# Routed experts of a mixture-of-experts layer: two output sums instead of one, and what is moved with them

## The chip, the cores and the metric

The kernel runs on one core of a Trainium2 chip. The metric is device time in microseconds (us) of one launch; the median of three runs of the kernel before is 2050.76 us (2043.1 to 2051.07). The kernel is written in an explicit form: each engine (TensorE for matmuls, VectorE, ScalarE and GpSimd for element work, SyncE for issuing DMAs) carries out its own list of instructions in order, and engines wait for each other and for DMAs on semaphores, which a tile layer derives from the reads and writes of each tile or DRAM tensor.

## The reference

One decoder layer on 1024 tokens of width 1024, all in float32: a mixing part (a state-space branch and a sparse-attention branch), and then a mixture of experts whose end is what the change touches:

```
scores = sigmoid(h @ w_router)               # 64 experts, top 8 of them per token, group-limited
w      = chosen scores / their sum * 2.5
for each expert e, for its tokens t:
    hid      = silu(h[t] @ w_gate[e]) * (h[t] @ w_up[e])      # 1024 -> 256
    routed[t] += (hid @ w_down[e]) * w[t, e]                   # 256 -> 1024
shared = (silu(h @ ws_gate) * (h @ ws_up)) @ ws_down
out    = x + gate_f * (routed + shared)
```

So every row of the output is a sum of ten terms: the residual x, the shared expert's row, and eight experts' rows.

## The kernel before

The sum is kept in the output tensor in DRAM itself. The mixing part writes x there. The shared expert's down projection (`job_down`, line 1735) works in eight groups of 128 rows and adds each group with a DMA that accumulates (line 1759). The routed experts (`moe`, line 2099) then add their rows one block at a time.

A block is up to 128 tokens of one expert. Experts are ranked by their number of tokens; a table (`SLOTS`, line 27) gives each rank one, two or three blocks of fixed sizes, 98 blocks in all: 38 of 128 rows, 12 of 64, 4 of 48, 26 of 88 to 120, and 18 of 32 rows or fewer (5 of 8, 5 of 16, 4 of 24, 4 of 32). `moe_order` (line 2026) puts seven experts with one block first, then mixes experts with one and with more blocks, and ends on the largest experts and three small ones. [...] The order within the loop is written out by hand (lines 2234 to 2273); for block b it is, on all engines together:

- `gu(b)`: gate and up projection on TensorE. Blocks over 64 rows use weights and tokens split in a high and a low part (three matmuls each, lines 253 to 255); smaller ones use plain float32 with the array cut into two or four column groups, so that two or four matmuls run beside each other (line 2169).
- `gather(b + 3)` (line 1858): an indirect DMA, issued by GpSimd, that brings the tokens of a later block into one of three buffers.
- `put(b - 2)`: VectorE multiplies the down projection's result with the token weights and the gate into one of two output buffers (line 2222; for up to 64 rows ScalarE first copies one half, line 2221), and GpSimd issues an indirect DMA that adds the rows to the output (line 2223, the scatter). Indices are distinct within one block but not between blocks, so each scatter waits until the one before has landed.
- `ht(b - 1)`: transposes of the hidden values (lines 2188 and 2191); `act(b)`: the SwiGLU (lines 2177 and 2178); `xpose(b + 2)`: transposes of the gathered tokens (lines 2141 and 2150); `dn(b - 1)`: the down projection (line 2210), four matmuls of 512 columns, for up to 64 rows in two column groups of the array.
- in between, the high and low parts of the next expert's weights (lines 2090 and 2091, on ScalarE and VectorE), and at the end of an expert the weight loads for three experts ahead (3 MB, lines 2068 and 2078, issued by SyncE).

GpSimd's list in this phase is therefore gather, scatter, gather, scatter, and it holds in order: a gather behind a scatter that waits is not issued either. Lists of each expert's tokens are still being made in the first blocks (`take` and `merge`), as much as the gathers of larger experts require.

Of the kernel before, what the change touches and what calls it, by code (L numbers as in the profile page):

```python
# [10 lines left out]
F32 = mybir.dt.float32  # L11
F32R = mybir.dt.float32r
BF = mybir.dt.bfloat16
I32 = mybir.dt.int32
AF = mybir.ActivationFunctionType
OP = mybir.AluOpType
# [4 lines left out]
P = 128  # L21
T = 1024
D = 1024
# [98 lines left out]
class Kernel:  # L122
# [1612 lines left out]
    def job_down(self):  # L1735

        nc, S = self.nc, self.sh
        ys = {}

        def grp(i, h):  # L1740
            def f(ws):
                ps = self.ps("mm", "mm")
                t = slice(i * P, (i + 1) * P)
                for j in range(2):
                    for k in range(2):
                        self.mm3(ps[:, 256 * j:256 * j + 256], S["hh"][:, k, t], S["hl"][:, k, t], *ws[4 * h + 2 * j + k],
                                 k == 0, k == 1)

                def after():
                    if h == 0:  # L1750
                        ys[i] = self.e1.tile([P, D], F32, name="y", **(dict(tag="mwT") if i % 3 == 2 else dict(tag="y", bufs=2)))
                    c = slice(512 * h, 512 * h + 512)
                    if h == 0:
                        nc.vector.tensor_tensor(ys[i][:, c], ps, self.r_gf[:, c], op=OP.mult)
                    else:
                        nc.scalar.copy(ys[i][:, c], ps)
                        nc.gpsimd.tensor_tensor(ys[i][:, c], ys[i][:, c], self.r_gf[:, c], op=OP.mult)
                    if h == 1:
                        nc.gpsimd.dma_start(self.out[i * P:(i + 1) * P], ys[i], accum_op=OP.add)
                return after  # L1760
            return f
        return (self.I["ws_down"], KT, 256, [grp(i + x, h) for i in range(0, KT, 2) for h in range(2) for x in range(2)])
# [336 lines left out]
    def moe(self):  # L2099
        nc, I, fp, rp = self.nc, self.I, self.fp, self.rp  # L2100
        v = nc.vector
        mm = nc.tensor.matmul
        W, order = self.W, self.order
        r4 = self.r4
        r3, gates = self.r3, self.gt

        c = 3 * (D + 64)
        self.spare, self.nov = r3[:64, c:c + 640], r3[:1, c + 640:c + 641].bitcast(I32)
        hT = self.qp.tile([P, 2, 2, P], F32, name="hT", tag="qb")
        xhs = [self.qp.tile([P, 4, 280], F32R, name="xh", tag="wraw", bufs=2) for _ in range(2)]  # L2110
        xhs = [x.rearrange("p k n -> p (k n)")[:, :D].rearrange("p (k n) -> p k n", k=KT) for x in xhs]
        ots = [r4[:, i * D:(i + 1) * D] for i in range(2)]
        self.keysF = r4[:64, 2 * D:3 * D]

        xss = [r4[:, 2 * D + 512 * i:2 * D + 512 * i + 512] for i in range(2)]
        nc.gpsimd.memset(r4[:, 2 * D:3 * D], 0.0)
        hids = self.hids = [r4[:, 3 * D + 256 * i:3 * D + 256 * i + 256] for i in range(2)]
        self.ov = r4[:1, 3 * D + 512:4 * D].bitcast(I32)
        wts, self.cols = [gates[:, i:i + 1] for i in range(6)], gates[:64, 8:24]
        gf = self.gf = self.r_gf  # L2120
        depth, nr = sum(QUOTA[0]), [sum(len(x) > q for x in QUOTA) for q in range(3)]
        r0, _ = self.first_ranks()
        bg = self.take(self.taken, depth) + [lambda: self.merge(depth, [(0, 0, r0), (1, 0, nr[1]), (2, 0, nr[2])])]
        tables = self.overflow_tables()
        bg, left = bg + tables, len(tables)
        blocks, B = self.blocks, self.B
        nb = len(blocks)
        def units(e):
            return [lambda k=k: self.gu_part(e, k, v) for k in range(len(W[e]["gu"]), KT)]

        def xpose(b):
            s = B[b]
            n, x = s["n"], s["x"]
            s["w"] = wts[b % 6][:n]
            v.tensor_copy(s["w"], x[:, D + s["r"]:D + s["r"] + 1])
            if n <= 64:
                m = s["m"] = 32 if n <= 32 else 64
                xs = xss[b % 2].rearrange("p (k n) -> p k n", k=KT)
                ps = self.ps("xt", "tp", [P, KT, 64])[:, :, :n]
                for k in range(KT):  # L2140
                    nc.tensor.transpose(ps[:, k], x[:, k:D:KT], self.ident[:n, :n])
                nc.scalar.copy(xs[:, :, :n], ps)
                s["st"] = [xs[:, k, :m] for k in range(KT)]
                return
            hi, lo = xhs[b % 2][:, :, :n], fp.tile([P, KT, P], F32R, name="xl", tag="xl", bufs=2)[:, :, :n]
            s["st"] = [(hi[:, k], lo[:, k]) for k in range(KT)]
            for q in range(2):
                ps = self.ps("xt", "tp", [P, 4, P])[:, :, :n]
                for k in range(4):
                    nc.tensor.transpose(ps[:, k], x[:, 4 * q + k:D:KT], self.ident[:n, :n])  # L2150
                ks = slice(4 * q, 4 * q + 4)
                nc.scalar.copy(hi[:, ks], ps)
                v.tensor_tensor(lo[:, ks], ps, hi[:, ks].bitcast(F32), op=OP.subtract)
# [46 lines left out]
        def dn(b):  # L2200

            s = B[b]
            n, w, st = s["n"], W[s["e"]]["dn"], s["hst"]
            if n > 64:
                s["o"] = [self.ps("o", "mm")[:n] for _ in range(2)]
            else:
                ps = self.ps("o", "mm")
                s["o"] = [ps[:n], ps[64:64 + n]]
            for k, h in [(k, h) for h in range(2) for k in range(2)] if n > 64 else [(k, h) for k in range(2) for h in range(2)]:
                mm(s["o"][h], st[:, k], w[:, k, 512 * h:512 * h + 512], start=k == 0, stop=k == 1)  # L2210

        def put(b):
            s = B.pop(b)
            n = s["n"]
            ot = ots[b % 2][:n]
            for h in (1, 0):
                c = slice(512 * h, 512 * h + 512)
                o = s["o"][h]
                if n <= 64 and h == 1:
                    o = ot[:, c]  # L2220
                    nc.scalar.copy(o, s["o"][1])
                v.scalar_tensor_tensor(ot[:, c], o, s["w"], gf[:n, c], op0=OP.mult, op1=OP.mult)  # L2222
            nc.gpsimd.indirect_dma_start(out=self.out, out_offset=bass.IndirectOffsetOnAxis(ap=s["ix"], axis=0),  # L2223
                                         in_=ot, in_offset=None, compute_op=OP.add)

        ne = len(order)
        xpose(0)
        for f in units(0):
            f()
        xpose(1)  # L2230
        for f in self.w_load(2, nc.sync):
            f()
        queue = []
        for b in range(nb + 2):
            if b < nb:
                e, r, q, n, first, last = blocks[b]
                if first:
                    assert not queue
                    if e + 1 < ne:
                        queue = units(e + 1)  # L2240
                    turns = len(QUOTA[r]) if e + 1 < ne else 1
                gu(b)
            if b + 3 < nb:
                while blocks[b + 3][1] < r0 and len(bg) > left:
                    bg.pop(0)()
                self.gather(b + 3)
            if 0 <= b - 2:
                put(b - 2)
            if b < nb:
                take = -(-len(queue) // max(turns, 1))  # L2250
                na = (take * 2 + 2) // 3
                for _ in range(na):
                    queue.pop(0)()
                if b > 0:
                    ht(b - 1)
                act(b)
                if b + 2 < nb:
                    xpose(b + 2)
                if b > 0:
                    dn(b - 1)  # L2260
                for _ in range(take - na):
                    queue.pop(0)()
                turns -= 1
                if last:
                    if e + 3 < ne:
                        for f in self.w_load(e + 3, nc.sync):
                            f()
                for _ in range(2 if 0 < b < self.rate[0] else b < self.rate[1] or b % 2):
                    if bg:
                        bg.pop(0)()  # L2270
            elif b == nb:
                ht(b - 1)
                dn(b - 1)
# [4 lines left out]
    def run(self):  # L2278
        nc, tc = self.nc, self.tc
        with ExitStack() as top:  # L2280
# [4 lines left out]
            self.d_u = self.dp.tile([512, T], F32, name="d_u")  # L2285
            self.d_ma = self.dp.tile([1024, T], F32, name="d_ma")
            self.d_h2 = self.dp.tile([T, D + 64], F32, name="d_h2")
            self.d_mask = self.dp.tile([64, T], F32, name="d_mask")
            self.fp = None
            self.idx0 = cp.tile([P, 64], I32, name="idx0")  # L2290
# [148 lines left out]
```

## Time and profile before

| what | value |
|---|---|
| median of three runs | 2050.76 us (2043.1 to 2051.07) |
| the profiled execution | 2056.37 us |
| its span, first to last instruction | 2054.6 us |
| mean granted TensorE clock | 0.963 |
| TensorE busy | 1910.8 us, 93% of the span |
| VectorE, ScalarE, GpSimd busy | 62%, 43%, 33% |
| bytes moved by DMA | 396 MB, mean 193 GB/s |

Busy TensorE is counted from the first to the modelled end of each matmul, and matmuls overlap, so "busy" says that it had work, not that it ran at its peak. The granted clock is a share of 2.4 GHz; a stretch between 0.5 and 1.0 has a part at 1.2 GHz. "Landing" of a DMA is the time from its issue until its semaphore says that all data are there. In the views, POOL is GpSimd, PE TensorE, DVE VectorE, ACT ScalarE, and a name such as `out<-ot,idx` gives the tensor written and those read (`idx` and `back` are two tables of token indices: those of an expert's first block, and of its later ones). A bracket `[9.46 <-DMA out<-ot,idx]` gives the idle time before an instruction and what ended it.

### The profile page before, as it was taken

The numbers are of one execution on the slowest core, as the hardware profiler recorded it, in microseconds if no ns is written. First come the engines' busy times: TensorE is split into PE (matmuls) and PEld (weight loads), VectorE is DVE, ScalarE is ACT, GpSimd is POOL, SyncE is SP. The second block draws the span as 40 slices with busy tenths as digits, with TensorE's granted clock in tenths as the row PEclk, the third lists the DMA queues.
The fourth block names the chain that finished last, engine by engine and source line by source line (L and its number), as shares of the span: only waits on it lengthen the run. The fifth ranks groups of instructions, "written<-read, shape, count | busy, mean of one in ns | idle before, by whom it ended". The sixth has DMA issues, their size and how long they took to land. (4 is left out here: it accounts for less than half of the span.)

```text
span 2054.6 us, 31808 instructions
## 1 busy us (share of the span) xinstructions
PE 1910.8 (93%) x11227; PEld 1381.7 (67%) x11227; DVE 1278.2 (62%) x2875; ACT 874.7 (43%) x2113; POOL 677.2 (33%) x706
## 2 busy tenths in 40 slices
PE   5997999999899999999898999999999999999897
PEld 4785887889866655688776565666666666666563
DVE  5740694256778886557778765656665655656454
ACT  5221224125667666333334444444444444444332
POOL 7524231222032111234436334433332323323231
PEclk9998999999979999999999999999999999999998
DMA  8327430731023210464349998898989989989984
GB/s 289 92 83 89 106 101 26 239 96 42 22 83 104 71 53 21 151 214 154 134 144 250 367 294 303 270 300 304 299 288 313 300 290 294 308 291 311 278 233 110
DMA packets 150420, 396.31 MB, mean 193 GB/s; under 512 B 22049, under 2 KB 89298, under 8 KB 125666
## 3 DMA queue, kind: packets, MB, share of 16 engines
q1 hardware_dynamic: 117330, 288.28, 40.1%
q0 software_dynamic: 25152, 87.10, 18.8%
q10 hardware_dynamic: 7776, 18.88, 2.5%
q8 instruction: 89, 1.46, 0.3%
q14 instruction: 73, 0.60, 0.1%
HBM read 328.27 MB, written 64.23 MB: 191 GB/s over the span
## 5 line engine op out<-in xcount | busy, mean ns | idle before, releaser
L289 POOL TENSOR_TENSOR wlo<-wraw,whi 128x256 fp32r<-128x256 f32 (+1 forms) x238 | 198.2, 854 | 435.8 <-ACT whi L288 428.1
L2091 DVE TENSOR_TENSOR gl<-raw,gh 128x512 fp32r<-128x512 f32 x508 | 325.4, 688 | 22.5 <-ACT gh L2090 22.2
L2210 PE MATMUL o<-rawdn,hT 128*128 128x512 f32 (+10 forms) x784 | 312.2, 628 | 4.6 <-ACT hT L2189 4.5
L2090 ACT CAST gh<-raw 128x512 fp32r<-128x512 f32 x512 | 280.8, 628 | 13.2 <-DMA raw<-in_w_gu 13.2
L2223 POOL DMA_INDIRECT out<-ot,idx x64 | 115.6, 1806 | 368.1 <-DMA out<-ot,idx 122.0
L253 PE MATMUL gu<-gh,xh 128*128 128x512 f32 (+5 forms) x512 | 220.1, 430 | 0.0
L2222 DVE SCALAR_TENSOR_TENSOR ot<-o,wts,r_gf 128x512 f32<-128x512 f32 (+11 forms) x162 | 115.0, 742 | 152.8 <-DMA out<-ot,idx 66.2
L254 PE MATMUL gu<-gl,xh 128*128 128x512 f32 (+5 forms) x512 | 202.5, 395 | 0.0
L255 PE MATMUL gu<-gh,xl 128*128 128x512 f32 (+5 forms) x512 | 202.3, 395 | 0.0
L2210 PEld LDWEIGHTS o<-rawdn,hT 128*128 128x128 f32 (+10 forms) x784 | 105.5, 164 | 132.5 <-issue 118.8
L255 PE MATMUL mm<-hT_hi,wlo 128*128 128x512 f32 x352 | 141.0, 401 | 18.1 <-POOL wlo L289 18.1
L288 ACT CAST whi<-wraw 128x256 fp32r<-128x256 f32 (+1 forms) x264 | 95.8, 405 | 138.4 <-DMA wraw<-in_w_in 44.4
L253 PE MATMUL mm<-hT_hi,whi 128*128 128x512 f32 x352 | 142.1, 404 | 0.3 <-ACT hT_hi L467 0.3
L254 PE MATMUL mm<-hT_lo,whi 128*128 128x512 f32 x352 | 140.1, 398 | 0.2 <-DVE hT_lo L474 0.2
L253 PEld LDWEIGHTS gu<-gh,xh 128*128 128x128 f32 (+5 forms) x512 | 93.0, 182 | 56.5 <-issue 33.1
L2223 POOL DMA_INDIRECT out<-ot,back x34 | 57.9, 1704 | 215.7 <-DMA out<-ot,idx 160.7
L254 PEld LDWEIGHTS gu<-gl,xh 128*128 128x128 f32 (+5 forms) x512 | 93.0, 182 | 31.9 <-issue 7.9
L255 PEld LDWEIGHTS gu<-gh,xl 128*128 128x128 f32 (+5 forms) x512 | 92.6, 181 | 27.0
L2169 PE MATMUL gu<-raw,ot 128*32 128x128 f32 (+1 forms) x1664 | 100.2, 312 | 0.0
L1332 POOL TENSOR_TENSOR p<-p,ms 128x384 f32<-128x384 f32 (+7 forms) x52 | 45.7, 895 | 165.2 <-DVE ms L1325 86.7
L1318 ACT ACTIVATE p<-p,ms 128x384 f32<-128x384 f32 (+7 forms) x128 | 85.9, 673 | 32.6 <-DVE ms L1312 32.2
L2189 ACT COPY hT<-ht 128x256 f32<-128x256 f32 (+5 forms) x64 | 22.8, 356 | 180.5 <-PE ht L2188 180.0
(580 smaller groups left out, 4166.4 us busy)
## 6 DMA issues: line engine op xcount, KB each, us to landing
raw<-in_w_gu SPq DMA_DIRECT2D x124, 1024.0 KB, 10.1
rawdn<-in_w_down SPq DMA_DIRECT2D x62, 1024.0 KB, 11.2
wraw<-in_w_ada SPq DMA_DIRECT2D x32, 512.0 KB, 3.7
wraw<-in_w_in SPq DMA_DIRECT2D x28, 512.0 KB, 4.3
ada<-in_w_ada SPq DMA_DIRECT2D x16, 512.0 KB, 8.5
d_th<-th ACTq DMA_DIRECT2D x32, 256.0 KB, 2.0
wraw<-in_w_out SPq DMA_DIRECT2D x16, 512.0 KB, 4.6
x<-in_x SPq DMA_DIRECT2D x8, 512.0 KB, 6.4
```

The costliest lines, as they stand in the source:

```text
L253: mm(ps, lh, rh, start=start, stop=False)
L254: mm(ps, lh, rl, start=False, stop=False)
L255: mm(ps, ll, rh, start=False, stop=stop)
L288: self.nc.scalar.copy(hi, raw)
L289: (eng or self.nc.gpsimd).tensor_tensor(lo, raw, hi.bitcast(F32), op=OP.subtract)
L1318: nc.scalar.activation(p, p, AF.Exp, scale=-1.0, bias=m[:, nch - 1, h:h + 1], accum_out=m[:, 3, h:h + 1])
L2090: self.nc.scalar.copy(hi, src)
L2091: eng.tensor_tensor(lo, src, hi.bitcast(F32), op=OP.subtract)
L2169: mm(ps[m * j:m * j + m, :2 * c].rearrange("p (s n) -> p s n", s=2), s["st"][k], w["raw"][k][:, :, a:min(a + 2 * c, 256):2], start=k == 0, ...
L2210: mm(s["o"][h], st[:, k], w[:, k, 512 * h:512 * h + 512], start=k == 0, stop=k == 1)
L2222: v.scalar_tensor_tensor(ot[:, c], o, s["w"], gf[:n, c], op0=OP.mult, op1=OP.mult)
L2223: nc.gpsimd.indirect_dma_start(out=self.out, out_offset=bass.IndirectOffsetOnAxis(ap=s["ix"], axis=0), in_=ot, in_offset=None, compute_op= ...
```

## The change

- The shared expert writes its rows plainly to a new DRAM tensor, `d_y2`, instead of adding them to the output.
- Routed blocks with an even number, up to block 92, add into `d_y2`; odd ones, and all after 92, into the output. Right behind block 92's scatter, one DMA adds all of `d_y2` to the output.
- There are three output buffers instead of two; the results of blocks 94 to 97 go to four buffers of their own, in a weight buffer that is no longer needed. The table of overflowing tokens moves to another tile to make room.
- Gathers are issued four blocks ahead instead of three; the number of gather buffers stays three.
- Down projections of blocks with 32 rows or fewer are cut into four column groups of 256 columns (eight matmuls) instead of two of 512. All 32 columns of the transposed hidden buffer are used, so that buffer is set to zero once. The four quarters are copied by ScalarE and scaled in one VectorE instruction of 1024 columns.

```diff
                     if h == 1:
-                        nc.gpsimd.dma_start(self.out[i * P:(i + 1) * P], ys[i], accum_op=OP.add)
+                        nc.gpsimd.dma_start(self.d_y2[i * P:(i + 1) * P], ys[i])
...
         hT = self.qp.tile([P, 2, 2, P], F32, name="hT", tag="qb")
+        nc.gpsimd.memset(hT, 0.0)
...
-        ots = [r4[:, i * D:(i + 1) * D] for i in range(2)]
+
+        ots = [r4[:, c:c + D] for c in (0, D, 3 * D + 512)]
...
-        self.ov = r4[:1, 3 * D + 512:4 * D].bitcast(I32)
+        self.ov = self.keys[:1].bitcast(I32)
...
             n, w, st = s["n"], W[s["e"]]["dn"], s["hst"]
+            if n <= 32:
+                ps = s["o"] = self.ps("o", "mm")
+                st = hT[:, b % 2, :, :32]
+                for k in range(2):
+                    for j in range(4):
+                        mm(ps[32 * j:32 * j + 32, :256], st[:, k], w[:, k, 256 * j:256 * j + 256], start=k == 0, stop=k == 1)
+                return
...
-            ot = ots[b % 2][:n]
-            for h in (1, 0):
+            ot = (ots[b % 3] if b < last2 + 2 else late[b - last2 - 2])[:n]
+            if n <= 32:
+                for j in range(4):
+                    nc.scalar.copy(ot[:, 256 * j:256 * j + 256], s["o"][32 * j:32 * j + n, :256])
+                v.scalar_tensor_tensor(ot, ot, s["w"], gf[:n], op0=OP.mult, op1=OP.mult)
+            for h in (1, 0) if n > 32 else ():
...
-            nc.gpsimd.indirect_dma_start(out=self.out, out_offset=bass.IndirectOffsetOnAxis(ap=s["ix"], axis=0),
-                                         in_=ot, in_offset=None, compute_op=OP.add)
+            nc.gpsimd.indirect_dma_start(out=self.d_y2 if b <= last2 and b % 2 == 0 else self.out, in_=ot, in_offset=None,
+                                         out_offset=bass.IndirectOffsetOnAxis(ap=s["ix"], axis=0), compute_op=OP.add)
+            if b == last2:
+                nc.gpsimd.dma_start(self.out, self.d_y2, accum_op=OP.add, max_dma_last_dim=4 * D)
...
+        last2 = nb - 6 - nb % 2
+        late = self.raw[(ne - 3) % 3].rearrange("p k s n -> p (k s n)")
+        late = [late[:, i * D:(i + 1) * D] for i in range(4)]
         xpose(0)
         for f in units(0):
             f()
+        self.gather(3)
         xpose(1)
...
-            if b + 3 < nb:
-                while blocks[b + 3][1] < r0 and len(bg) > left:
+            if b + 4 < nb:
+                while blocks[b + 4][1] < r0 and len(bg) > left:
                     bg.pop(0)()
-                self.gather(b + 3)
+                self.gather(b + 4)
...
+            self.d_y2 = self.dp.tile([T, D], F32, name="d_y2")
```

## Rows read from the trace of the kernel before

**Rows 1.** Busy time by stretch: us; PE, PEld, DVE, ACT, POOL busy; PEclk, DMA share, GB/s.
```profile
1200.00:1950.00 750.00, 713.53 (x4167) 460.16 (x4166) 451.85 (x830) 337.26 (x744) 251.19 (x159) 0.98 0.91 295
...
2012.00:2054.60 42.60, 28.16 (x106) 15.02 (x104) 16.41 (x29) 9.09 (x22) 8.37 (x5) 0.87 0.38 77
```
**Rows 2.** The same view in stretches of 10 us.
```profile
1820.00:1830.00 10.00, 10.00 (x47) 6.71 (x47) 5.63 (x10) 5.84 (x12) 3.09 (x2) 1.00 1.02 367
...
1940.00:1950.00 10.00, 6.45 (x24) 3.31 (x25) 6.60 (x12) 2.39 (x6) 2.44 (x2) 0.83 0.98 297
1950.00:1960.00 10.00, 10.00 (x47) 6.44 (x47) 4.99 (x9) 3.88 (x9) 4.96 (x4) 1.00 0.83 217
```
**Rows 3.** TensorE's waits, 1200 to 1950 us: total us, times, longest.
```profile
PE xt L2150 <- DMA xg<-d_h,idx: 22.4, 17, 3.2
PE xt L2141 <- DMA xg<-d_h,back: 11.6, 7, 4.0
```
**Rows 4.** GpSimd's waits in the same stretch.
```profile
POOL out L2223 <- DMA out<-ot,idx: 266.2, 40, 9.8
POOL out L2223 <- DMA out<-ot,back: 70.0, 13, 7.8
```
**Rows 5.** DMA issues in the same stretch: count, median us from issue to landing.
```profile
out<-ot,idx POOLq DMA_INDIRECT x50, 9.6
...
out<-ot,back POOLq DMA_INDIRECT x29, 7.2
```
**Rows 6.** GpSimd in order of time: start us, us, line, operation, idle before.
```profile
1928.29 1.58 POOL L2223 DMA_INDIRECT out<-ot,idx  x1 [4.58 <-DMA out<-ot,idx]
1930.18 1.51 POOL L1858 DMA_INDIRECT xg<-d_h,back  x1 [0.30 <-PE xt L2150]
1941.15 1.44 POOL L2223 DMA_INDIRECT out<-ot,back  x1 [9.46 <-DMA out<-ot,idx]
```
**Rows 7.** TensorE in order of time, the wait at 1940 us.
```profile
1943.55 1.07 PE L2141 MATMUL xt<-ident,xg 64*128 64x64 f32 x8 [3.96 <-DMA xg<-d_h,back]
```
**Rows 8.** TensorE in order of time: three steps of blocks of 112, 16 and 16 rows.
```profile
1401.26 3.60 PE L2210 MATMUL o<-rawdn,hT 128*112 128x512 f32 x8
1404.79 2.02 PE L2169 MATMUL gu<-raw,ot 128*32 128x128 f32 x64
...
1418.15 1.90 PE L2210 MATMUL o<-rawdn,hT 128*16 128x512 f32 x8
```
**Rows 9.** ScalarE's copies by shape, 1200 to 1950 us: count, busy us, mean ns, idle before.
```profile
L2189 ACT COPY hT<-ht 128x256 f32<-128x256 f32 x34 | 12.7, 372 | 95.2 <-PE ht L2188 94.8
...
L2221 ACT COPY ot<-o 16x512 f32<-16x512 f32 x5 | 2.9, 578 | 13.6 <-DMA out<-ot,idx 10.3 <-DMA out<-ot,back 3.3
```
**Rows 10.** Shared expert's end: waits of ScalarE and TensorE, landing of adds and plain writes.
```profile
ACT y L1756 <- DMA out<-y: 8.7, 2, 6.0
...
PE mm L253 <- ACT y L1756: 6.9, 3, 4.5
...
DMA to landing us min/median/max: 5.2/7.7/12.0
...
d_h<-h POOLq DMA_DIRECT2D x4, 512.0 KB, 3.3
```
**Rows 11.** The end in order of time: block 92 scaled and scattered, the last scatter.
```profile
2002.10 1.41 DVE L2222 SCALAR_TENSOR_TENSOR ot<-o,wts,r_gf 128x512 f32<-128x512 f32 x2 [1.78 <-PE o L2210]
...
2004.75 1.59 POOL L2223 DMA_INDIRECT out<-ot,idx  x1 [4.46 <-DVE gl L2091]
...
2046.05 1.57 POOL L2223 DMA_INDIRECT out<-ot,idx  x1 [5.51 <-DVEq L1964]
```
**Rows 12.** Landing of scatters: 64 and 88 rows near the end; all, min/median/max.
```profile
out<-ot,back POOLq DMA_INDIRECT x1, 5.7
...
out<-ot,idx POOLq DMA_INDIRECT x1, 6.2
...
DMA to landing us min/median/max: 3.1/8.4/12.1
```

## The prediction

> **What bounds the kernel now.** I read the busy times by stretch first. Of the 2054.6 us the routed experts take about 950, and their even middle, 1200 to 1950 us, is what the change touches most: TensorE is busy 713.5 of 750 us at a granted clock of 0.98, the DMA engines 0.91 of the time [rows 1]. So TensorE is the bound there, with 36.5 us idle and 0.02 x 750 = 15 us lost to the lower clock level, and the DMA engines stand close behind: a stretch in which they are full reads 1.02 in the same column (367 GB/s), so their work would fit in 0.91 x 750 / 1.02 = 669 us [rows 1, 2].
>
> Then the waits. Almost all of TensorE's attributed waiting in the middle is for gathered tokens: 22.4 + 11.6 = 34.0 us in 24 waits, the longest 4.0 [rows 3]. The clock loss is the same thing again: the 10 us with the 3.96 us wait read 0.83, a part of them at 1.2 GHz, and the next 10, without a wait, 1.00 [rows 2, 7]. Gathers are late because of GpSimd's order. It issues gather, scatter, gather, scatter, and each scatter waits for the landing of the one before, as both add into the output: 266.2 + 70.0 us of waiting [rows 4]. Landing takes 9.6 us in the median for first blocks of an expert and 7.2 for the later ones; 50 x 9.6 + 29 x 7.2 = 689 of the 750 us are such a chain [rows 5]. One case in full: the scatter issued at 1928.29 lets the next go only at 1941.15; the gather between them was issued at 1930.18, and TensorE, idle from 1939.6 on, got its tokens at 1943.55 [rows 6, 7].
>
> At the end it is different. From 2012 us on, the DMA engines are 0.38 busy, TensorE has 28 us of work left, and the span closes with the last scatters, one after the other [rows 1, 11].
>
> **The change, part by part.** The sum is made against the profiled execution, 2056.4 us (span 2054.6 and 1.8 around it), which stands 5.6 above the median of 2050.8.
>
> *Shared expert: plain write instead of add.* Eight writes of 512 KB that add take 7.7 us to land (5.2 to 12.0), a plain one of that size 3.3; ScalarE waited 8.7 us for these buffers and TensorE 6.9 us behind ScalarE, 4.5 in the wait that follows the longest one [rows 10]. Gain between 0 and 6.9; I take 4, a little under that one wait.
>
> *Two chains and gathers four ahead.* Even blocks add into the second tensor, so a scatter waits for the one two blocks back: about 17 us of block time against a landing of 9.6, and the wait of rows 4 should mostly go. The gather moves one block forward in GpSimd's order (750 us / 79 scatters = 9.5 us per block), and no wait of TensorE for a gather exceeds 4.0 us. Its buffer (three remain) was last read by the transposes of block b+1, done one block before. What is late next is the scaled output on VectorE, which GpSimd waits for and nobody else. Worth: 36.5 us idle and 15 us of clock at most, 51.5 together.
>
> *Third output buffer.* VectorE and ScalarE wait less for old scatters; TensorE's share of that is already in the idle time, so nothing is added.
>
> *Quartered down projection.* 18 of the 98 blocks have 32 rows or fewer. Their down projection now takes 1.90 us, half of the 3.60 of a full block, because two column halves of the array run beside each other [rows 8]. In quarters, four run beside each other: 8 matmuls of 256 columns stream a quarter of 3.60, 0.90 us, and 16 records at the pace of the quartered gate/up step (64 in 2.02 us) issue in 0.5. I take 1.0, so 18 x 0.9 = 16 us. Bounds: 0, if the quarters gain nothing over halves, and 18 x 1.0 = 18.
>
> *Evacuation of these blocks.* Four ScalarE copies of 256 columns, 0.37 each at 128 rows, instead of one of 0.578: +0.9 us a block, 16 in all [rows 9]. ScalarE is busy 337 of 750 us [rows 1], and that idle time hides it; uncovered, 16 us, which would cancel the quarters.
>
> *Sum of the middle.* TensorE's floor is 750 - 51.5 - 16 = 682.5 us, that of the DMA engines 669. At 98% load weights and gathers will be late now and then, more so as experts with a single block need as much weight traffic for less TensorE work. Bounds of the gain are 15 (little more than the quarters) and 67; I take two thirds, 45.
>
> *The memset of the transposed buffer, the moved overflow table, the earlier merge of the token lists:* below 1 us on GpSimd, nothing, and two rounds brought forward by one block; 0, with 5 us either way.
>
> *The end.* Block 92 is the last that adds into the second tensor. Its result is scaled by 2003.5 us; scattered at once and landed after 9.6, that is 2013.4 [rows 5, 11]. Behind it GpSimd issues one DMA that adds the second tensor, 4 MB in 1024 rows of 4 KB, to the output. It must wait for that scatter, and the five scatters left (two of 64 rows, three of 88) go to the output, must wait for it, and then for each other. No row shows an add from DRAM to DRAM. Nearest are the eight adds of 128 rows and the quiet scatters of the end. With the 3.1 us of the quickest scatter as fixed part, the quickest add gives (5.2 - 3.1) / 128 = 0.016 us a row, 20 us in all; the quiet 88-row scatter (6.2 - 3.1) / 88 = 0.035, 39 us; the slowest add under load, 12.0, gives 0.070 and 74 [rows 10, 12]. I take 29, between the two quiet ones, and keep 20 and 74. So: 2013.4 + 0.3 + 29 = 2042.7; two scatters of 0.3 + 5.7, three of 0.3 + 6.2: 2074.2; and the 2.3 us that now follow the last landing (2046.05 + 6.2 against 2054.6): 2076.5 [rows 11, 12]. That is 22 us later than now, because those scatters today run beside TensorE's last 28 us and then all stand behind the add. The spare buffers keep VectorE and TensorE from waiting, but the chain itself is the end.
>
> A rule of the Trainium skill bears on this price. Rows 10 and 12 show 20 to 39 us for such an add; "DMA: Bandwidth & Descriptors", section "Anatomy of one DMA — SWDGE (gpsimd) path", fits a transfer from GpSimd as 2 us plus the bytes over 436 GB/s, which for 4.19 MB would be an estimated 11.6 us. By that rule the end would cost 5 us instead of 22. The rows of this case disagree for adds: 512 KB would be 3.2 us by it, near the plain write's 3.3, and the quickest add took 5.2.
>
> Total: -4 - 45 + 22 = -27, so 2029.4 in the terms of this profile, 2024 in those of the median.
>
> **Rivals.**
> 1. *The DMA engines take over.* The gathers come on time, but weights don't, and only the quarters and a little more remain, or the two chains still wait for each other: 20 of the middle's 67 us. For it: 0.91 of the time busy already, and 1.02 in the stretch of rows 2; against it: SyncE's loads go out two experts ahead. -4 - 20 + 22 = -2: 2049.
> 2. *All of the middle is won.* For it: every wait is shorter than the block by which the gather moves. -4 - 67 + 22: 2002.
> 3. *Slower: the add of the second tensor.* At the pace of the slowest add, 74 us, the end moves by 67 and not 22: -4 - 45 + 67 = +18, 2069. It decides from an add of 66 us on (29 + 27 + 10). For it: both sides of this add lie in DRAM, and it meets the last weights. Against it: from 2012 us the DMA engines are 0.38 busy.
> 4. *A quick add.* It streams as fast as the DMA engines move anything here, 367 GB/s [rows 2]: 3.1 + 4.19 MB / 367 GB/s = 14.5 us, and the end costs 7.5: -4 - 45 + 7.5 = -41, 2009. For it: nothing else wants the engines then; against it: no add in rows 10 or 12 comes near that rate. (By the rule of the Trainium skill above it would be 2007.)
>
> **How the numbers follow.** Chances: forecast 0.45, rival 1 0.20, rival 2 0.13, rival 3 0.13, rival 4 0.09. Half a percent, 10 us, is about what a measurement of this kernel can tell from no change. Faster by more takes nearly all of the forecast (0.42), rivals 2 and 4 and a little of rival 1: 0.66. Slower takes rival 3 and the worst of rival 1: 0.16. The rest, 0.18, is within. The range runs from rival 2 with an add of 20 us (1993, rounded to 1995) to rival 1 with an add of a few us more (2054). The forecast's own range, 30 to 60 us from the middle and 20 to 39 from the add, is 2000 to 2049.
>
> **What would show it.** Right: TensorE's wait for gathered tokens under 10 us in the middle, its clock near 1.00, the scatters' wait for landings a fraction of 336 us, the small blocks' down projection near 1.0 us, DMA share near 0.97. Right at the end: one long gap on GpSimd of 25 to 40 us and five scatters on the chain that ends last. Wrong: TensorE waiting for weights instead, an add far outside 20 to 39 us, or small blocks still at 1.9.

## The result and the profile after

The changed kernel takes 2001.66 us (1998.89 to 2003.82, four runs) against 2049.44 us before: a ratio of 0.9766 with a 95% interval of 0.9744 to 0.9788, 48 us. The profiled execution has a span of 1998.7 us, 55.9 less than that of before; the profile of before lay above its median, so the traces show a few us more than the runs.

TensorE's middle first: busy time by stretch, with the columns of [rows 1]. The middle that took until 1950 us now ends near 1875.

```profile
1200.00:1910.00 710.00, 706.92 (x4416) 474.47 (x4415) 467.39 (x842) 362.48 (x827) 272.12 (x168) 1.00 0.99 322
1910.00:1960.00 50.00, 49.10 (x238) 28.98 (x237) 26.86 (x50) 18.76 (x43) 7.63 (x5) 1.00 0.94 236
1960.00:1998.70 38.70, 6.01 (x16) 2.04 (x14) 2.81 (x4) 0.31 (x1) 7.61 (x5) 0.61 0.37 57
```

TensorE is idle 3 us of 710 where it was idle 36.5 of 750, its clock is 1.00, and the same DMA engines move 322 GB/s instead of 295. Its waits of [rows 3] are gone; the one that is left is new (transposed hidden values, late behind ScalarE's extra copies):

```profile
PE o L2219 <- ACT hT L2191: 3.1, 5, 0.7
```

GpSimd, from 1200 to 1910 us, hardly waits for landings any more (9.6 us in all, against the 336 of [rows 4]) but for results to scatter, and each scatter still takes as long to land as in [rows 5], or longer:

```profile
POOL d_y L2236 <- DVE ot L2235: 96.1, 35, 3.8
POOL out L2236 <- DVE ot L2235: 89.4, 31, 3.7
```
```profile
d_y<-ot,idx POOLq DMA_INDIRECT x27, 11.6
out<-ot,idx POOLq DMA_INDIRECT x26, 11.6
out<-ot,back POOLq DMA_INDIRECT x16, 8.1
d_y<-ot,back POOLq DMA_INDIRECT x15, 9.1
```

The down projection of the small blocks, which answers to [rows 8], went from 1.90 to 1.07 us:

```profile
1414.47 1.07 PE L2211 MATMUL o<-rawdn,hT 128*32 128x256 f32 x16
```

And the end, GpSimd in order of time, which answers to [rows 11]: block 92's scatter at 1928.74, the addition of the second sum 11 us later, a gap of 23.59, and then the five scatters, each behind the one before.

```profile
1928.74 1.77 POOL L2236 DMA_INDIRECT d_y<-ot,idx  x1 [6.75 <-DVE ot L2235]
1940.06 1.42 POOL L2239 DMA_DIRECT2D out<-d_y  x1 [9.55 <-DMA d_y<-ot,idx]
1965.07 1.48 POOL L2236 DMA_INDIRECT out<-ot,back  x1 [23.59 <-issue]
1970.55 1.40 POOL L2236 DMA_INDIRECT out<-raw,back  x1 [4.01 <-issue]
1976.06 1.59 POOL L2236 DMA_INDIRECT out<-raw,idx  x1 [4.10 <-issue]
1983.08 1.57 POOL L2236 DMA_INDIRECT out<-raw,idx  x1 [5.44 <-issue]
1990.23 1.57 POOL L2236 DMA_INDIRECT out<-raw,idx  x1 [5.58 <-issue]
```

ScalarE's activation, one per block, marks the time through the whole phase. The rows are those of block 8 and block 90, first of before, then of after:

```profile
1206.02 0.23 ACT L2177 ACTIVATE ot<-gu 128x64 f32<-128x64 f32 x1
...
1971.63 0.28 ACT L2177 ACTIVATE ot<-gu 128x128 f32<-128x128 f32 x1
```
```profile
1200.30 0.23 ACT L2179 ACTIVATE ot<-gu 128x64 f32<-128x64 f32 x1
...
1896.58 0.28 ACT L2179 ACTIVATE ot<-gu 128x128 f32<-128x128 f32 x1
```

So 5.7 us are won up to block 8, 69.3 between blocks 8 and 90, nothing from there to block 97, and 19 are given back at the end (from block 97's activation to the end of the span 21.2 before, 40.4 after). Below, "the middle" is this stretch from block 8 to block 90: 765.6 us before, 696.3 after. In the traces of the changed kernel and of the seven variants below that have two sums, quarters and no added loads, or 256 KB of them, it lies between 696.3 and 698.7, while block 8 starts anywhere from 1193 to 1205. Of the kernel before there is one trace, of a run 7 us above its median, so gains against its middle may be that much too large.

### The profile page after: what moved, and what is told of

It reads as the page before. It is cut to its first block, busy times and chain, and to the rows that moved or that the text cites. A ratio compares the mean times of both kernels' runs of the same rounds, so it can differ in the third digit from the quotient of the medians.

```text
span 1998.7 us, 32103 instructions
## 1 busy us (share of the span) xinstructions
PE 1871.2 (94%) x11359; PEld 1374.8 (69%) x11371; DVE 1273.0 (64%) x2857; ACT 886.0 (44%) x2167; POOL 691.8 (35%) x708
## 5 line engine op out<-in xcount | busy, mean ns | idle before, releaser
L2219 PE MATMUL o<-rawdn,hT 128*128 128x512 f32 (+7 forms) x640 | 265.4, 601 | 6.7 <-ACT hT L2191 6.7
L2219 PEld LDWEIGHTS o<-rawdn,hT 128*128 128x128 f32 (+7 forms) x640 | 96.8, 174 | 116.1 <-issue 101.0
L2235 DVE SCALAR_TENSOR_TENSOR ot<-o,wts,r_gf 128x512 f32<-128x512 f32 (+7 forms) x137 | 96.9, 744 | 75.2 <-PE o L2219 75.2
L2180 DVE TENSOR_TENSOR ot<-ot,gu 128x256 f32<-128x256 f32 (+7 forms) x98 | 35.2, 359 | 150.6 <-ACT ot L2179 140.5
L1858 POOL DMA_INDIRECT xg<-d_h,idx x64 | 68.1, 1064 | 172.2 <-issue 88.0
L2236 POOL DMA_INDIRECT d_y<-ot,idx x31 | 67.5, 2178 | 93.7 <-DVE ot L2235 91.1
## 6 DMA issues: line engine op xcount, KB each, us to landing
raw<-in_w_gu SPq DMA_DIRECT2D x124, 1024.0 KB, 10.5
```

Of the source, the lines that this page charges most:

```text
L1858: self.nc.gpsimd.indirect_dma_start(out=x, out_offset=None, in_=self.d_h2, in_offset=bass.IndirectOffsetOnAxis(ap=ix, axis=0))
L2236: nc.gpsimd.indirect_dma_start(out=self.d_y2 if b <= last2 and b % 2 == 0 else self.out, in_=ot, in_offset=None, out_offset=bass.IndirectO ...
```

## The experiments

Two theories of the middle stood against each other. W: gathers were too late, and a lead of one more block mends that. C: the one chain of landings bounds the middle, and whatever is given more lead or room, the wait only shows elsewhere.

**One sum.** Everything of the change but the second sum; the shared expert adds to the output again.

```diff
-                        nc.gpsimd.dma_start(self.d_y2[i * P:(i + 1) * P], ys[i])
+                        nc.gpsimd.dma_start(self.out[i * P:(i + 1) * P], ys[i], accum_op=OP.add)
...
-            nc.gpsimd.indirect_dma_start(out=self.d_y2 if b <= last2 and b % 2 == 0 else self.out, in_=ot, in_offset=None,
+            nc.gpsimd.indirect_dma_start(out=self.out, in_=ot, in_offset=None,
...
-            if b == last2:
-                nc.gpsimd.dma_start(self.out, self.d_y2, accum_op=OP.add, max_dma_last_dim=4 * D)
```

> The changed kernel, but every block adds into the output and nothing is added at the end; gathers four ahead, three buffers and quarters stay. Theory W (the gain is the lead of the gathers: no wait of TensorE exceeded 4.0 us and the gather moves by a whole block): the middle keeps its 69 us, the 20 us at the end come back, the shared expert's adds cost 3: about 1985. Theory C (the chain of landings is a bound by itself: 50 x 9.6 + 29 x 7.2 us, and 0.3 us before each next issue, make 713 us where the changed kernel took 681): the middle loses 32 of its 69 us: about 2017, with GpSimd waiting for landings nearly all the time and TensorE waiting for something behind it.

Measured: 2029.24 us (2017.96 to 2038.63), ratio to before 0.9874 [0.9831, 0.9917]; in the trace, of the slowest of the four runs, the middle wins 24 us of the 69. W falls by 44 us, and by 33 for the fastest run. C's number is missed too, by 12, but its mechanism holds: with the landings of this trace the chain makes 52 x 10.3 + 30 x 6.7 = 737 of the 741.6 us between blocks 8 and 90. TensorE still waits for tokens, with gathers a block earlier, because GpSimd still sits behind landings (1200 to 1910 us):

```profile
PE xt L2152 <- DMA xg<-d_h,idx: 33.8, 13, 5.0
```
```profile
POOL out L2236 <- DMA out<-ot,idx: 220.8, 28, 9.8
...
POOL out L2236 <- DMA out<-ot,back: 42.7, 10, 6.7
```

**Four ahead alone.** The kernel before, with the lead and nothing else.

```diff
+        self.gather(3)
...
-            if b + 3 < nb:
-                while blocks[b + 3][1] < r0 and len(bg) > left:
+            if b + 4 < nb:
+                while blocks[b + 4][1] < r0 and len(bg) > left:
...
-                self.gather(b + 3)
+                self.gather(b + 4)
```

> The kernel before with gathers four ahead and nothing else. Theory C (the one chain of landings bounds the middle): the run with one sum won 23 us in all, some 10 of them by the quarters, so at most 13 are left for lead and buffers: 2037 to 2050. Theory W (lead): the 34 us of waiting and 15 us of clock go: 2000 to 2005.

Measured: 2051.62 us, ratio 0.9998 [0.9981, 1.0016], so nothing. The trace is the best picture of C. TensorE's waits for gathered tokens are all gone, and 30.0 us of another wait stand there. It comes from ScalarE, which waits for the two output buffers, which wait for landings (1200 to 1910 us):

```profile
PE o L2210 <- ACT hT L2189: 30.0, 15, 4.3
```
```profile
ACT ot L2221 <- DMA out<-ot,idx: 72.2, 14, 9.2
...
ACT ot L2221 <- DMA out<-ot,back: 26.1, 6, 5.3
```

Scatters start 9.2 us apart on average between blocks 8 and 90, against 9.3 in the kernel before. This trace is of the fastest of ten runs; its middle is 752.5 us, 13 less than that of the one trace of before, although the runs show no difference. So the middle of a kernel with one chain can't be read from one trace more closely than that. Nor is a sum of median landings always a good gauge of the chain: here the medians are 6.4 and 6.5 us, which would make only 528 us, and the spacing of the scatters is the surer sign.

**Three ahead.** The changed kernel without the fourth block of lead.

```diff
-        self.gather(3)
...
-            if b + 4 < nb:
-                while blocks[b + 4][1] < r0 and len(bg) > left:
+            if b + 3 < nb:
+                while blocks[b + 3][1] < r0 and len(bg) > left:
...
-                self.gather(b + 4)
+                self.gather(b + 3)
```

> The changed kernel with gathers three ahead as before. Theory C: with two chains GpSimd no longer sits behind a landing, gathers go out on time anyway, and the fourth block of lead adds nothing: 2002 within 3. Theory W: the lead is what counts, and landings of 10 to 13 us in full DMA queues bring back a part of the 34 us of waiting and 15 us of clock: 2012 to 2040.

Measured: 2001.92 us, ratio 0.9775 [0.9738, 0.9811], like the changed kernel. With two chains the lead adds nothing; TensorE's waits for tokens come to 1.1 us in 710.

**Two buffers.** The changed kernel with two output buffers.

```diff
-        ots = [r4[:, c:c + D] for c in (0, D, 3 * D + 512)]
+        ots = [r4[:, c:c + D] for c in (0, D)]
...
-            ot = (ots[b % 3] if b < last2 + 2 else late[b - last2 - 2])[:n]
+            ot = (ots[b % 2] if b < last2 + 2 else late[b - last2 - 2])[:n]
```

> The changed kernel with two output buffers. A buffer comes free after a landing of 11.6 us and is wanted after two blocks, 17 us, so the third buffer should be worth nothing: 2002 within 3. If pairs of a large and a small block make the two-block distance shorter than the landing, ScalarE and VectorE wait there again and the next expert's weights are late: 2005 to 2020.

Measured: 2002.16 us, ratio 0.9755 [0.9734, 0.9777]. Beside two sums, the third buffer is worth nothing either.

**Two sums alone.** The kernel before with what the two sums need.

```diff
-                        nc.gpsimd.dma_start(self.out[i * P:(i + 1) * P], ys[i], accum_op=OP.add)
+                        nc.gpsimd.dma_start(self.d_y2[i * P:(i + 1) * P], ys[i])
...
-            ot = ots[b % 2][:n]
+            ot = (ots[b % 2] if b < last2 + 2 else late[b - last2 - 2])[:n]
...
-            nc.gpsimd.indirect_dma_start(out=self.out, out_offset=bass.IndirectOffsetOnAxis(ap=s["ix"], axis=0),
-                                         in_=ot, in_offset=None, compute_op=OP.add)
+            nc.gpsimd.indirect_dma_start(out=self.d_y2 if b <= last2 and b % 2 == 0 else self.out, in_=ot, in_offset=None,
+                                         out_offset=bass.IndirectOffsetOnAxis(ap=s["ix"], axis=0), compute_op=OP.add)
+            if b == last2:
+                nc.gpsimd.dma_start(self.out, self.d_y2, accum_op=OP.add, max_dma_last_dim=4 * D)
...
+        last2 = nb - 6 - nb % 2
+        late = self.raw[(ne - 3) % 3].rearrange("p k s n -> p (k s n)")
+        late = [late[:, i * D:(i + 1) * D] for i in range(4)]
...
+            self.d_y2 = self.dp.tile([T, D], F32, name="d_y2")
```

> The kernel before with the two sums, their addition near the end and the last four buffers, but with two output buffers, gathers three ahead and halves. Theory C: all of the middle but the quarters' 10 us comes from here, and the end costs its 20: 2010 to 2017, with GpSimd waiting for results and not for landings. If the third buffer is needed with two scatters in flight: results wait for landings of 11.6 us, gathers behind them, and part of TensorE's waiting stays: 2020 to 2040.

Measured: 2013.78 us, ratio 0.98 [0.9771, 0.9829], and the middle wins 56.2 of the 69.3 us. So the second sum is nearly the whole gain but for the quarters (10.5, next run); the lead and the third buffer are left with 2.6 us by the traces and 1 by the runs.

**No quarters.** The changed kernel with the old down projection of small blocks.

```diff
-            if n <= 32:
+            if n < 0:
                 ps = s["o"] = self.ps("o", "mm")
...
-            if n <= 32:
+            if n < 0:
                 for j in range(4):
...
-            for h in (1, 0) if n > 32 else ():
+            for h in (1, 0):
```

> The changed kernel with down projections of 32 rows or fewer in halves, as before. If TensorE is the bound of the middle: 18 x (1.90 - 1.07) = 15 us more, 2017. If the DMA engines, at a share of 0.99, are: no difference, 2002.

Measured: 2012.64 us, ratio 0.9817 [0.9788, 0.9846], 11 us more than the changed kernel, and 10.5 in the middle (58.8 against 69.3). TensorE is the bound: it is busy all the time from block 8 to block 90. The quarters' 18 x 0.83 would be 15 us; 3 of them go into the new wait for ScalarE that is shown above and is absent here, the rest I can't place. The stretch from block 8 to block 90 before, without quarters, and in the changed kernel:

```profile
1206.02:1971.63 765.61, 729.14 (x4210) 469.72 (x4209) 459.19 (x843) 342.12 (x756) 259.60 (x165) 0.98 0.91 293
```
```profile
1200.03:1906.84 706.81, 706.81 (x4206) 463.64 (x4206) 459.55 (x841) 339.57 (x756) 265.23 (x165) 1.00 0.98 318
```
```profile
1200.30:1896.58 696.28, 693.20 (x4350) 465.38 (x4350) 457.16 (x823) 353.41 (x809) 265.14 (x165) 1.00 0.99 322
```

**No last addition.** The second sum is left out of the output.

```diff
-            if b == last2:
-                nc.gpsimd.dma_start(self.out, self.d_y2, accum_op=OP.add, max_dma_last_dim=4 * D)
```

> The changed kernel without the last addition of the second sum to the output, which so lacks that sum. If the add and the five scatters behind it set the end: the last scatter goes out right after the last block is scaled, 75 us earlier than in the kernel before, and the time is 1980 to 1984. If the add only takes time that the last blocks need anyway: 2002.

Measured: 1981.04 us, ratio 0.9665 [0.9635, 0.9694]. The end costs 20.6 us. The last scatter goes out 3 us after the last block is scaled (1963.86 + 1.40), because it still waits for the landing of the one before it, 7 us apart, as in the kernel before:

```profile
1963.86 1.40 DVE L2235 SCALAR_TENSOR_TENSOR raw<-o,wts,r_gf 88x512 f32<-88x512 f32 x2 [2.90 <-PE o L2219]
```
```profile
1961.26 1.59 POOL L2236 DMA_INDIRECT out<-raw,idx  x1 [8.23 <-DVE raw L2235]
1968.36 1.59 POOL L2236 DMA_INDIRECT out<-raw,idx  x1 [5.51 <-DVEq L1964]
```

**Rows of 8 KB** in the last addition.

```diff
-                nc.gpsimd.dma_start(self.out, self.d_y2, accum_op=OP.add, max_dma_last_dim=4 * D)
+                nc.gpsimd.dma_start(self.out, self.d_y2, accum_op=OP.add, max_dma_last_dim=8 * D)
```

> The changed kernel whose last addition goes in rows of 8 KB instead of 4 KB, half as many. If its 24.2 us go with the number of rows: 14 us, 1992. If they go with the bytes (4.19 MB at 214 GB/s with the DMA engines 0.99 busy): no difference, 2002 within 3.

Measured: 2003.76 us, ratio 0.9764 [0.9742, 0.9785], and the addition still lands after about 24 us (1943.32 to the next scatter's issue at 1967.76, against 25.0 from issue to issue in the changed kernel), although the packets of GpSimd's DMAs in the 30 us around it fall from 1130 to 615. So it doesn't go with the number of rows. That it goes by bytes is what is left, and no run with other bytes shows it.

**Block 94 as the last** that adds into the second sum.

```diff
-        last2 = nb - 6 - nb % 2
+        last2 = nb - 4 - nb % 2
```

> The changed kernel with block 94 instead of 92 as the last that adds into the second sum, so that three scatters and not five stand behind the last addition. The addition starts two blocks later, some 11 to 13 us after 1940, and two scatters of 5.5 us less follow it: no difference, 2002 within 4. If the end goes by the number of scatters behind it: 1990.

Measured: 2006.88 us, ratio 0.9779 [0.9743, 0.9815]: no gain, and 5 us above 2002 where 4 were allowed. In the trace the stretch from block 97's activation to the end is 43.0 us against 40.4. The addition lands after 24.7 us and starts 13 us later against block 92's scatter; the two scatters saved are worth about 11. (The rest of the difference in time lies in the start, before block 8.)

Then the question on which my sum had turned: are the DMA engines full at a share of 0.99?

**Half the down weights.** Every second expert's load of `w_down` is left out.

```diff
-            eng.dma_start(t, I["w_down"][bass.ds(st["x"], 1)].rearrange("a (p k) n -> p (a k) n", p=P))
+            if e < 4 or e % 2 == 0:
+                eng.dma_start(t, I["w_down"][bass.ds(st["x"], 1)].rearrange("a (p k) n -> p (a k) n", p=P))
```

> The changed kernel without the load of the down-projection weights for every second expert from the fifth on (old weights are used in their place), some 30 MB less. If the DMA engines, 0.99 busy, still cost the middle something: 10 to 40 us faster. If TensorE alone is the bound, with 3 us of waiting left in 710: 2002 within 4, and only the DMA share falls, to about 0.88.

Measured: 2001.12 us, ratio 0.9761 [0.9725, 0.9797]. The DMA engines cost the middle nothing: it takes 696.3 us, as with all weights. Note the share: bytes fall by 11%, the share by 7.

**Loads nobody reads**, 256 and 512 KB an expert, into the room of the third output buffer. The edit is made on the changed kernel with two buffers, whose two lines stand above; the larger load is 1024 columns wide instead of 512.

```diff
+                        if e >= 5:
+                            nc.sync.dma_start(r4[:, 3 * D + 512:3 * D + 512 + 512],
+                                              I["w_gu"][e + 3].rearrange("(p k) n -> p (k n)", p=P)[:, :512])
```

> The changed kernel with two output buffers (2002), where SyncE also loads 256 KB that nobody reads for each expert from the sixth on: 55 x 262 KB = 14.4 MB, 39 us of full DMA engines at 367 GB/s. If a share of 0.99 means that the engines are full: their floor of 669 us becomes 708 against TensorE's 681, so about 27 us more, 2029. If the share overstates it and there is room: 2002 within 4.

> The same with 512 KB for each expert: 28.8 MB, 79 us. Full engines: 669 + 79 = 748 against 681, 67 us more, 2069. Room for it: 2002 within 4. Between the two: the difference to the run with 256 KB tells the price of a further MB.

Measured: 1998.59 us with 256 KB, ratio 0.9754 [0.9706, 0.9803], no loss; 2023.54 with 512 KB, ratio 0.9864 [0.9829, 0.9899], 21 us more than with two buffers alone. From block 8 to block 90 it is 696.6 and 719.8 us, against 697.5 with two buffers. The middle (1200 to 1910 us) by share and rate, half the down weights, 256 and 512 KB:

```profile
1200.00:1910.00 710.00, 706.96 (x4440) 475.02 (x4432) 467.41 (x842) 361.45 (x826) 272.58 (x168) 1.00 0.92 285
```
```profile
1200.00:1910.00 710.00, 706.59 (x4419) 475.93 (x4418) 465.34 (x836) 358.31 (x819) 269.58 (x167) 1.00 1.02 341
```
```profile
1200.00:1910.00 710.00, 691.72 (x4290) 463.04 (x4290) 452.93 (x814) 353.88 (x801) 252.14 (x163) 0.99 1.03 351
```

With 256 KB ScalarE waits 1.4 us in all for weights. Only in the last do they come late, and there ScalarE says so at once:

```profile
ACT gh L2090 <- DMA raw<-in_w_gu: 82.7, 33, 7.1
```

At 1.02 the engines still had room. Whether they are full at 351 GB/s is not shown, because the added loads all go to one buffer and make a chain themselves: each waits for the landing of the one before, and SyncE's list, with the weight loads in it, stands behind that wait, with 256 and then with 512 KB:

```profile
SPq L2289 <- DMA ot<-in_w_gu: 206.4, 47, 11.2
```
```profile
SPq L2289 <- DMA ot<-in_w_gu: 483.3, 50, 14.0
```

So the 21 us may be the price of that chain, of full engines, or of both. The rate is a bound all the same: at 351 GB/s the middle of before, 295 GB/s over 750 us, is at most 630 us of work and not 669.

## Why the prediction came out as it did

The direction was right and the time lay within the range, at its lower part, 22 us below the forecast of 2024. In number it is the second rival, 2002, to which I had given 0.13; but that rival's reason, that every wait is shorter than the block by which the gather moves, is theory W, and the lead alone changed nothing. So that its number came out is partly luck. By steps:

- *The bound.* I named TensorE as the bound and the chain of landings behind GpSimd as the reason for its waits. The chain is more than that: with the lead alone TensorE's waits for tokens go and the time stays, so the chain itself bounds the middle of before, as 689 of 750 us [rows 5] could have told. TensorE is the bound only once there are two chains.
- *Which edit mends it.* I gave the two chains and the lead one sum together. The runs part them: the second sum brings 56 of the 69 us, the lead and the third buffer nothing beside it, and the lead alone 0.
- *36.5 us of idle time and 15 of clock.* They came in but for 3 us idle: clock 1.00, no wait for tokens. With the quarters' 10 that makes 58 to 62; the middle won 69.3, some 8 us more. They lie in TensorE's busy time: for the same matmuls TensorE is busy 729.1 us before in the run without quarters 706.8. That is 22 us less, of which the clock explains 15; what made up the rest stays open. By the runs there is less to explain: 48 us, and the 20.6 of the end, less 3 to 6 of the start, leave 63 to 65 for the middle.
- *The quarters.* 1.07 us against the 1.0 taken; 10.5 us of the 16; 3 of the rest are the wait for ScalarE, whose idle time didn't cover the copies in full. (The lower bound of the middle's gain, 15, is called a little more than the quarters, but is a little less than their 16.)
- *Two thirds of the middle, 45.* This is the step that failed. I took the DMA engines' floor as 669 us from a busy share, 0.91 against 1.02, put it beside TensorE's 682.5, and discounted the gain for it. The middle won all of the 67 I had as the ceiling, or nearly all by the runs. The share isn't a measure of room: 322 GB/s pass without a late weight at 0.99, and 341 at 1.02 with 1.4 us of waiting for weights.
- *The end.* 22 us predicted, 19 in the trace and 20.6 by leaving the addition out. The addition took 24.2 us, within 20 to 39 and below the 29 taken; the gap on GpSimd was 23.6, a little under the 25 to 40 named as its sign. Block 92 landed after 10.8, and the five scatters took the time summed for them. By the rule of the Trainium skill ("DMA: Bandwidth & Descriptors", section "Anatomy of one DMA — SWDGE (gpsimd) path") the addition would take an estimated 11.6 us; the measured 24.2 differ from it and decide.
- *The plain write.* Landing 3.8 us instead of 7.7; TensorE's wait behind ScalarE fell from 6.9 to 4.1, and block 0 comes 3.2 us earlier. That agrees with 4 but doesn't show it, as block 0 moves by 8 us among the traces with the plain write (1107.7 to 1116.0, the changed kernel 1112.9, before 1116.1).

Sum as it came out in the traces: -5.7 - 69.3 + 19.2 = -55.8, against -27.

## What to carry to other kernels

Where updates of one tensor must follow each other, look at the chain of landings first: if their sum, or the spacing of the updates, fills the stretch, that chain is the bound, whichever engine shows the wait, and more lead only moves the wait along. (A third buffer alone beside one chain was not run.) A second place to add to halves the chain and costs one pass over the tensor, plus every update that has to stand behind that pass; reckon the end by it. And don't discount a gain by a busy share of the DMA engines: look for a consumer that waits for a transfer. The rate alone is no scale either, as it depends on what is moved: the last addition reads a share of 1.06 at 211 GB/s.

```profile
1944.50:1961.00 16.50, 15.60 (x58) 8.73 (x57) 7.02 (x12) 3.77 (x10) 0.00 (x0) 1.00 1.06 211
```

## What the runs showed of the hardware

- The DMA share reads 0.92 at 285 GB/s, 0.99 at 322, 1.02 at 341 and 1.03 at 351. From 0.99 on, 6% more were moved without loss of time; 9% more came with a loss of 21 us, beside a chain of loads on SyncE that may be its cause.
- An addition of 4.19 MB from DRAM to DRAM took 24.2 us in rows of 4 KB, 173 GB/s of added data with little beside it, and about as long in rows of 8 KB.
- Four column groups of 256 columns took 1.07 us where two of 512 took 1.90; half of that is 0.95.
